# Weight blocks stored two by two, column by column, and a pad tile of 64 instead of 128 bytes

## The chip, the cores and the metric

The kernel runs on one core of one Trainium2 chip. The metric is the device time of one execution in microseconds (us). The profile names five engines: PE (TensorE, the matrix unit, whose weight loads have a row PEld of their own), DVE (VectorE), ACT (ScalarE), POOL (GpSimd) and SP (SyncE, which here only issues DMAs).

## The reference, cut to what matters

Two transformer-like blocks of two layers each, on 256 tokens of width 1024, all in float32. What matters for this change is that nearly all the work is the product of activations with large weight matrices:

```python
for l in range(2):                                   # first block
    proj = rmsnorm(x, ...) @ w_in[l]                 # 1024 -> 6656: q k v g, conv inputs, gates
    y_ret, y_sc, y_cf = retention(...) @ w_ret_out[l], conv3(...) @ w_sc_out[l], conv31(...) @ w_cf_out[l]
    x = x + rmsnorm((g0*y_ret + g1*y_sc + g2*y_cf) @ w_o[l], ...)
    gate, val = split(conv3(rmsnorm(x, ...) @ w_up[l]))       # 1024 -> 2 * 2816
    x = x + rmsnorm((silu(gate) * val) @ w_down[l], ...)      # 2816 -> 1024
for l in range(2):                                   # second block
    z = rms(x, ...) @ w_in_2[l]                      # mLSTM, sparse attention, differential attention, gates
    x = x + merged(...) @ w_out_2[l]
    x = x + (silu(g) * u) @ w_down_2[l]              # g, u = split(rms(x, ...) @ w_gate_up_2[l])
```

## The kernel before, in words

Activations lie transposed: 128 partitions hold 128 features, and the 256 tokens run along the free dimension. All weights are cut on the host into blocks of 128 by 128, in the very order in which the kernel uses them (`plan`, `pack_weights`), and packed into one array `stream` of chunks of eight blocks (128 x 1024 float32, 512 KB). `Weights` loads a chunk into `wraw` by one DMA on SP's queue (line 307). ACT rounds it into `whi` (float32r, line 326), and DVE forms the rest `wlo = wraw - whi` (line 328, recorded at line 417). Four buffers each of `wraw`, `whi` and `wlo`.

`job` walks over the plan. For a job of kind "B" each weight block is the stationary operand and the 256 tokens of one slice of the activations move past it: three matmuls of 128x256 a block (whi with the high part of the activations, whi with the low part, wlo with the high part: `hh`/`hl`, `yh`/`yl`, `fh`/`fl` in the profile), each with its own weight load, summed in PSUM. Four chunks (`WHOLE`) are used as plain float32, with one matmul a block that shows as two instructions. For a job of kind "A" (the values v, mv, dv and the up-projected values of the sparse attention) the roles are turned round: the activations are loaded and four weight blocks move past, 512 columns at once; it takes four blocks together (`take(4)`), kind "B" takes them singly:

```python
    def take(self, n=1):
        c, b = divmod(self.cur, CB)
        assert b + n <= CB
        self.cur += n
        s = slice(b * P, (b + n) * P)
        return [y[:, s] for y in self.parts[c]]
```

So before, block b of a chunk is the contiguous 128 columns b*128 to b*128+127 (512 bytes in each partition), and consecutive columns of the block are 4 bytes apart.

The order of the instructions on each engine comes from a scheduler that sees the jobs and, between them, side tasks (convolutions, attention, norms) which `side` hands out by estimated PE and DVE time. Tiles are given addresses in the order in which the pools are made: weights, constants, then the pool "state" (`xpool`), whose first tile `xpad` (line 365) is never used; its 128 bytes only move what is allocated after it: `x`, `hh`, `hl`, `yh`, `yl` and all pools behind. As the built program has them, every weight block of `whi`, `wlo` and `wraw` begins 128 bytes after a multiple of 256, and every slice of `hh`, `hl`, `yh`, `yl`, `fh`, `fl` begins 64 bytes after one.

Of the kernel before, what the change touches and what calls it, by code (L numbers as in the profile page):

```python
# [11 lines left out]
F32 = mybir.dt.float32  # L12
# [5 lines left out]
P = 128  # L18
# [108 lines left out]
def pack_weights(inputs):  # L127
    blocks = []
    cache = {}
    for arr, idx, kind, nk, cols in plan():  # L130
        key = (arr, idx)
        if key not in cache:
            cache[key] = np.asarray(inputs[arr])[idx]
        w = cache[key]
        if kind == "B":
            c = np.concatenate(cols)
            t = w[:, np.maximum(c, 0)]
            if (c < 0).any():
                t = np.where(c[None, :] < 0, np.zeros_like(t), t)
            n = len(cols)  # L140
            blocks.append(t.reshape(nk, P, n, P).transpose(0, 2, 1, 3).reshape(nk * n, P, P))
        else:
            t = w[:, cols].reshape(nk, P, 4, P).transpose(0, 2, 1, 3).reshape(nk * 4, P, P)
            blocks.append(t)
    n = sum(b.shape[0] for b in blocks)
    tot = -(-n // CB) * CB
    out = np.zeros((tot // CB, P, CB, P), np.float32)
    i = 0
    for b in blocks:
        for j in range(b.shape[0]):  # L150
            out[(i + j) // CB, :, (i + j) % CB, :] = b[j]
        i += b.shape[0]
    return out.reshape(tot // CB, P, CW)
# [59 lines left out]
def make_consts():  # L213

    off, parts = {}, []
    pos = 0

    def add(name, a):
        nonlocal pos
        a = np.asarray(a, np.float32)  # L220
        if a.shape[0] < P:
            a = np.concatenate([a, np.zeros((P - a.shape[0],) + a.shape[1:], np.float32)])
        a = a.reshape(P, -1)
        off[name] = (pos, a.shape[1])
        pos += a.shape[1]
        parts.append(a)

    add("ident", np.eye(P))
    inv = (np.float32(1.0) / np.power(np.float32(10000.0), np.arange(0, 64, 2, dtype=np.float32) / np.float32(64))).astype(np.float32)
    ang = np.arange(T, dtype=np.float32)[None, :] * inv[:, None]  # L230
    cos = np.cos(ang.astype(np.float64)).astype(np.float32)
    sin = np.sin(ang.astype(np.float64)).astype(np.float32)
    add("cos", np.tile(cos, (4, 1)))
    add("sin", np.concatenate([-sin, sin, -sin, sin]))
    i = np.arange(P)
    add("causb", np.where(i[None, :] > i[:, None], NEG, 0.0))
    e4 = np.zeros((P, 4, 4))
    for h in range(4):
        e4[:, h, h] = 1.0 / P
    add("st4", e4)  # L240
    s8 = np.zeros((P, 4, 8))
    for t in range(4):
        s8[:64, t, 2 * t] = 1.0 / 64
        s8[64:, t, 2 * t + 1] = 1.0 / 64
    add("st8", s8)
    hm = np.zeros((P, 2))
    hm[:64, 0] = 1.0 / 64
    hm[64:, 1] = 1.0 / 64
    add("hm2", hm)
    sel = np.zeros((P, 3, 4))  # L250
    for h in range(4):
        sel[64 + h, 0, h] = 1.0
        sel[68 + h, 1, h] = 1.0
        sel[72 + h, 2, h] = 1.0 / 16
    add("sel", sel)
    return off, pos, np.concatenate(parts, axis=1)
# [26 lines left out]
class Weights:  # L283
# [5 lines left out]
    def __init__(self, g, stream):  # L289
        self.g, self.stream = g, stream  # L290
        self.n = stream.shape[0]
        self.raw, self.parts = {}, {}
        self.loaded = self.conv = 0
        self.cur = 0
        self.whole = whole_chunks()
        self.first = False
# [39 lines left out]
    def take(self, n=1):  # L336
        c, b = divmod(self.cur, CB)
        assert b + n <= CB
        self.cur += n
        s = slice(b * P, (b + n) * P)  # L340
        return [y[:, s] for y in self.parts[c]]


class Gen:
    SLACK = 4000

    def __init__(self, ctx, tc, aps):
        self.ctx, self.tc, self.nc = ctx, tc, tc.nc
        self.aps = aps
        nc = self.nc  # L350
        PS = bass.MemoryType.PSUM
        self.wpool = ctx.enter_context(tc.tile_pool(name="weights", bufs=1))
        self.cpool = ctx.enter_context(tc.tile_pool(name="consts", bufs=1))
        self.xpool = ctx.enter_context(tc.tile_pool(name="state", bufs=1))
        self.dram = ctx.enter_context(tc.tile_pool(name="dram", bufs=1, space=bass.MemoryType.DRAM))
        self.psum = ctx.enter_context(tc.tile_pool(name="psum", bufs=1, space=PS))
        self.jobs = iter(plan())
        self.norms = 0
        self.tasks, self.later = [], []
        self.pe = self.dve = 0  # L360
        self.t_x = [None]
        self.urgent = {}
        self.idle = None

        self.xpool.tile([P, 32], F32, name="xpad")
        self.x = self.xpool.tile([P, KD, T], F32, name="x")
        xin = aps["x"].rearrange("p (k t) -> p k t", k=KD)
        self.coff, nco, _ = make_consts()
        self.cst = self.cpool.tile([P, nco], F32, name="cst")
        self.poff, npr, _ = pack_params()  # L370
        self.prm = self.cpool.tile([P, npr], F32, name="prm")
        self.g0 = self.cpool.tile([P, KD], F32, name="g0")
        o = self.poff["norm_mix_pre", 0][0]
        nc.scalar.dma_start(self.g0, aps["params"][:, o:o + KD])
        self.ones = self.cpool.tile([P, T], F32, name="ones")
        nc.vector.memset(self.ones, 1.0)
        self.eps = self.cpool.tile([P, 1], F32, name="eps")
        nc.vector.memset(self.eps, EPS)
        self.warm = self.cpool.tile([P, 1], F32, name="warm")
        self.act(self.warm, self.eps, AF.Square)  # L380
        self.W = Weights(self, aps["stream"])
        for i in range(4):
            nc.sync.dma_start(self.x[:, 2 * i:2 * i + 2], xin[:, 2 * i:2 * i + 2])
            self.W.load_to(i + 1)
        nc.sync.dma_start(self.prm, aps["params"])
        nc.sync.dma_start(self.cst, aps["consts"])
# [1250 lines left out]
```

## Time and profile before

| | |
|---|---|
| time, median of 3 runs | 1784.51 us (1778.77 to 1785.51) |
| the profiled execution | 1783.79 us, of which span 1782.1 us |
| PE busy | 1770.8 us, 14462 matmul instructions |
| PEld busy | 1723.9 us, 14462 weight loads |
| DVE busy | 1360.8 us |
| ACT busy | 1110.6 us |
| POOL busy | 69.7 us |
[...]
| DMA | 322.52 MB, mean 181 GB/s |

A matmul's record runs from its start to a modelled end, and consecutive records overlap: one of 128x256 lasts about 0.28 us, yet they start some 0.115 us apart. What counts is therefore the distance from start to start, called the pace below, and not the duration or the busy share. A row of the chain of waits that merges many matmuls gives it: its time divided by its count.

### The profile page before, as it was taken

What the parts mean: (1) busy time and instruction counts of PE and PEld (TensorE: products, weight loads), DVE (VectorE), ACT (ScalarE), POOL (GpSimd) and SP (SyncE); (2) the same over time, 40 slices, a digit from 0 to 9 for tenths busy, and PEclk for the clock granted to TensorE, in tenths of its full rate; (3) what the DMA queues carried; (4) which work ended last, traced back from release to release, by engine and by line L of the source; (5) the groups of instructions that cost most, each with busy time, mean ns of one, the idle gap of its engine ahead of it and who ended that gap; (6) DMA issues with size and microseconds to landing.
All of it is one profiled execution on the core that took longest, in us unless ns stands there. A gap on an engine that the chain in (4) does not pass through costs nothing.

```text
span 1782.1 us, 35765 instructions
## 1 busy us (share of the span) xinstructions
PE 1770.8 (99%) x14462; PEld 1723.9 (97%) x14462; DVE 1360.8 (76%) x2082; ACT 1110.6 (62%) x1787; POOL 69.7 (4%) x144
## 2 busy tenths in 40 slices
PE   8999999999999999999999999999999999999999
PEld 8999999999999999999998999999999999999999
DVE  8998689866999779883988877855569887687553
ACT  7676568755666568764676666644457666655442
POOL 0000000000000000000022100000001210000000
PEclk9999999999999999999999999999999999999999
DMA  7655545555555545555555644555555664455553
GB/s 269 195 177 187 191 143 202 190 189 172 200 177 190 180 149 195 190 189 166 164 191 181 210 133 146 190 185 187 188 185 172 202 196 137 144 188 189 188 189 121
DMA packets 94648, 322.52 MB, mean 181 GB/s; under 512 B 12257, under 2 KB 16913, under 8 KB 94482
## 3 DMA queue, kind: packets, MB, share of 16 engines
q1 hardware_dynamic: 91010, 314.15, 53.1%
q0 software_dynamic: 3328, 6.09, 1.2%
q8 instruction: 113, 1.85, 0.4%
q14 instruction: 53, 0.43, 0.1%
q10 hardware_dynamic: 144, 0.00, 0.0%
HBM read 312.80 MB, written 1.10 MB: 176 GB/s over the span
## 4 chain that ended last, share of the span: by engine, by line
PE 97%; DVE 1%; DMA 1%; issue 1%; ACT 0%; POOL 0%; SPq 0%; DVEq 0%; ACTq 0%; POOLq 0%
PE acc L405 90%; PE sp L405 6%; PE sp L410 1%; DMA Wm<-rows 0%; DMA tmp<-dq 0%; DMA x<-x 0%; DVE sc L1169 0%; DVE x L417 0%; DVE m L1168 0%; DVE yw L422 0%; DVE wlo L417 0%; ACT sd L447 0%; DVE dq L417 0%; ACT whi L326 0%; DVE Wm L428 0%
## 5 line engine op out<-in xcount | busy, mean ns | idle before, releaser
L326 ACT ACTIVATE whi<-wraw 128x1024 fp32r<-128x1024 f32 (+1 forms) x575 | 606.5, 1057 | 529.6 <-PE acc L405 359.6
L417 DVE TENSOR_TENSOR wlo<-wraw,whi 128x1024 fp32r<-128x1024 f32 (+1 forms) x575 | 697.0, 1218 | 285.9 <-ACT whi L326 284.8
L405 PE MATMUL acc<-hh,whi 128*128 128x256 f32 x2832 | 791.4, 280 | 0.0
L405 PE MATMUL acc<-hl,whi 128*128 128x256 f32 x2832 | 791.0, 280 | 0.0
L405 PE MATMUL acc<-hh,wlo 128*128 128x256 f32 x2832 | 789.8, 280 | 0.0
L405 PEld LDWEIGHTS acc<-hh,whi 128*128 128x128 f32 x2832 | 534.0, 189 | 5.5 <-issue 3.7
L405 PEld LDWEIGHTS acc<-hh,wlo 128*128 128x128 f32 x2832 | 534.4, 189 | 1.1 <-issue 0.8
L405 PEld LDWEIGHTS acc<-hl,whi 128*128 128x128 f32 x2832 | 532.0, 188 | 1.9 <-issue 1.2
L405 PE MATMUL acc<-yh,whi 128*128 128x256 f32 x1280 | 268.5, 283 | 6.1 <-ACT whi L326 6.1
L405 PE MATMUL acc<-yh,wlo 128*128 128x256 f32 x832 | 230.8, 282 | 0.0
L405 PEld LDWEIGHTS acc<-yh,whi 128*128 128x128 f32 x1280 | 210.4, 190 | 6.9 <-ACT whi L326 6.1
L405 PE MATMUL acc<-fh,wlo 128*128 128x256 f32 x704 | 197.9, 281 | 0.0
L405 PE MATMUL acc<-fl,whi 128*128 128x256 f32 x704 | 197.7, 281 | 0.0
L405 PE MATMUL acc<-fh,whi 128*128 128x256 f32 x704 | 197.5, 281 | 0.0
L405 PEld LDWEIGHTS acc<-yh,wlo 128*128 128x128 f32 x832 | 156.7, 190 | 0.4
L405 PEld LDWEIGHTS acc<-fh,wlo 128*128 128x128 f32 x704 | 133.6, 190 | 0.0
L405 PEld LDWEIGHTS acc<-fh,whi 128*128 128x128 f32 x704 | 133.5, 190 | 0.0
L405 PEld LDWEIGHTS acc<-fl,whi 128*128 128x128 f32 x704 | 132.2, 188 | 0.0
L405 PE MATMUL acc<-yl,whi 128*128 128x256 f32 x384 | 107.5, 281 | 0.0
L405 PEld LDWEIGHTS acc<-yl,whi 128*128 128x128 f32 x384 | 72.2, 188 | 0.2
L447 ACT ACT_TABLE_LOAD x50 | 64.2, 1283 | 5.3 <-DVE Wm L428 2.8
L422 DVE SCALAR_TENSOR_TENSOR up<-z,prm,up 128x254 f32<-128x254 f32 (+1 forms) x128 | 55.1, 476 | 0.0
(282 smaller groups left out, 1812.1 us busy)
## 6 DMA issues: line engine op xcount, KB each, us to landing
wraw<-stream SPq DMA_DIRECT2D x581, 512.0 KB, 3.4
kr<-rows SPq DMA_DIRECT2D x32, 64.0 KB, 3.1
dec<-decay SPq DMA_DIRECT2D x2, 768.0 KB, 4.2
x<-x SPq DMA_DIRECT2D x4, 256.0 KB, 6.2
rf<-rows SPq DMA_DIRECT2D x8, 128.0 KB, 3.6
tmp<-dq POOLq DMA_DIRECT2D x16, 64.0 KB, 2.9
Wm<-rows SPq DMA_DIRECT2D x8, 128.0 KB, 3.2
tmp<-dk POOLq DMA_DIRECT2D x16, 64.0 KB, 4.0
```

The lines of the kernel that those rows point to most:

```text
L326: nc.scalar.activation(h[:, s], r[:, s], AF.Copy)
L405: return self.nc.tensor.matmul(out, lhsT, rhs, start=start, stop=stop, **kw)
L410: return self.nc.tensor.transpose(out, in_, self.c("ident")[:k, :k])
L417: self.recent = self.nc.vector.tensor_tensor(out=out, in0=a, in1=b, op=op)
L422: return self.nc.vector.scalar_tensor_tensor(out, a, s, b, op0=op0, op1=op1)
L447: return self.nc.scalar.activation(out, in_, f, **kw)
```

## The change

Three edits.

1. `pack_weights` lays the blocks of kind "B" out in pairs: in the 256 columns that two consecutive blocks take up, column 0 of the first block is followed by column 0 of the second, then column 1 of each, and so on. Blocks of kind "A" stay as they were. The bytes, chunks and DMAs are the same.
2. `take`, when it hands out a single block, gives every second column of the pair: 128 columns that are 8 bytes apart, spread over 1024 bytes instead of 512. The second block of a pair begins 4 bytes after the first.
3. The unused tile `xpad` has 64 bytes instead of 128, so that everything behind it moves down by 64 bytes. The slices of `hh`, `hl`, `yh`, `yl`, `fh`, `fl` now begin at a multiple of 256; the weight buffers stay where they were. From the start of the weights to the start of the activations it was 192 bytes modulo 256; it is 128 for the first block of a pair and 124 for the second.

In the compiled program a weight load's pattern starts at the last column of the block and steps down: by one element before, by two now. The moving operand steps up by one element in both.

No engine's instructions change their order, their number or their waits: on PE, DVE, ACT, POOL and SP the lists of both programs agree row by row, up to line numbers.

```diff
@@ pack_weights @@
             n = len(cols)
-            blocks.append(t.reshape(nk, P, n, P).transpose(0, 2, 1, 3).reshape(nk * n, P, P))
+
+            t = t.reshape(nk, P, n, P).transpose(0, 2, 1, 3).reshape(nk * n // 2, 2, P, P)
+            blocks.append(t.transpose(0, 2, 3, 1).reshape(-1, P, 2, P).transpose(0, 2, 1, 3).reshape(-1, P, P))
@@ Weights.take @@
         self.cur += n
+        if n == 1:
+
+            s = slice((b & ~1) * P, (b | 1) * P + P)
+            return [y[:, s].rearrange("p (c h) -> p h c", h=2)[:, b & 1] for y in self.parts[c]]
         s = slice(b * P, (b + n) * P)
         return [y[:, s] for y in self.parts[c]]
@@ Gen.__init__ @@
-        self.xpool.tile([P, 32], F32, name="xpad")
+        self.xpool.tile([P, 16], F32, name="xpad")
```

## Rows read from the trace of the kernel before

**Rows 1.** The page: busy time of the engines, and the chain's shares
```profile
PE 1770.8 (99%) x14462; PEld 1723.9 (97%) x14462; DVE 1360.8 (76%) x2082; ACT 1110.6 (62%) x1787; POOL 69.7 (4%) x144
PE 97%; DVE 1%; DMA 1%; issue 1%; ACT 0%; POOL 0%; SPq 0%; DVEq 0%; ACTq 0%; POOLq 0%
```

**Rows 2.** The chain of waits, merged pieces: start us, us, what, count
```profile
113.00 43.18 PE acc L405 x379
...
165.13 66.31 PE acc L405 x563
...
246.80 177.61 PE acc L405 x1508
...
533.46 50.66 PE acc L405 x445
...
593.51 58.06 PE acc L405 x493
...
667.05 177.61 PE acc L405 x1508
...
1135.80 173.37 PE acc L405 x1472
...
1545.23 51.59 PE acc L405 x455
...
1599.29 179.15 PE acc L405 x1521
```

**Rows 3.** The page's costliest groups: matmuls of kind "B", count, busy us, mean ns
```profile
L405 PE MATMUL acc<-hh,whi 128*128 128x256 f32 x2832 | 791.4, 280 | 0.0
L405 PE MATMUL acc<-yh,whi 128*128 128x256 f32 x1280 | 268.5, 283 | 6.1 <-ACT whi L326 6.1
L405 PE MATMUL acc<-yh,wlo 128*128 128x256 f32 x832 | 230.8, 282 | 0.0
L405 PE MATMUL acc<-fh,wlo 128*128 128x256 f32 x704 | 197.9, 281 | 0.0
L405 PE MATMUL acc<-yl,whi 128*128 128x256 f32 x384 | 107.5, 281 | 0.0
```

**Rows 4.** Groups of PE from 560 to 580 us
```profile
L405 PE MATMUL acc<-hh,whi 128*128 128x256 f32 x59 | 16.1, 276 | 0.0
```

**Rows 5.** Groups of PE from 700 to 720 us
```profile
L405 PE MATMUL acc<-hh,whi 128*128 128x256 f32 x57 | 16.0, 281 | 0.0
```

**Rows 6.** Timeline from 1007.5 us: sixteen weight loads, each with a matmul of 2 columns
```profile
1007.42 1.87 PEld L405 LDWEIGHTS sp<-cst,sqt 128*128 128x128 f32 x16
1007.53 1.84 PE L405 MATMUL sp<-cst,sqt 128*128 128x2 f32 x16
```

**Rows 7.** Timeline of PE from 425 us: plain float32 matmuls (start us, us)
```profile
425.54 1.46 PE L405 MATMUL acc<-ones 128*128 128x256 f32 x6
```

**Rows 8.** Timeline of PE from 44 us: kind "A", 512 columns (start us, us)
```profile
44.04 0.39 PE L405 MATMUL acc<-whi,hh 128*128 128x512 f32 x1
...
46.33 0.39 PE L405 MATMUL acc<-wlo,hh 128*128 128x512 f32 x1
```

**Rows 9.** Windows: us, busy us of PE, PEld, DVE, ACT, POOL, clock, DMA share, GB/s
```profile
260.00:440.00 180.00, 179.75 (x1481) 178.00 (x1481) 136.90 (x217) 121.93 (x206) 0.20 (x1) 1.00 0.54 183
440.00:480.00 40.00, 40.00 (x296) 37.89 (x296) 38.79 (x56) 26.84 (x40) 3.93 (x8) 1.00 0.63 209
480.00:600.00 120.00, 120.00 (x1026) 117.75 (x1025) 113.97 (x160) 76.84 (x112) 0.51 (x1) 1.00 0.56 182
860.00:900.00 40.00, 39.99 (x294) 37.35 (x292) 38.22 (x59) 25.05 (x36) 4.02 (x8) 1.00 0.62 203
1320.00:1360.00 40.00, 40.00 (x315) 38.46 (x314) 37.54 (x58) 25.76 (x35) 3.99 (x8) 1.00 0.59 197
```

**Rows 10.** The page's costliest groups: forming `whi` and `wlo`
```profile
L326 ACT ACTIVATE whi<-wraw 128x1024 fp32r<-128x1024 f32 (+1 forms) x575 | 606.5, 1057 | 529.6 <-PE acc L405 359.6
L417 DVE TENSOR_TENSOR wlo<-wraw,whi 128x1024 fp32r<-128x1024 f32 (+1 forms) x575 | 697.0, 1218 | 285.9 <-ACT whi L326 284.8
```

## The prediction, written before the changed kernel ran

> **What bounds the kernel now.** I read the page's busy shares and the chain's shares first. PE holds 97% of the chain and is busy for 99% of the span [rows 1], so only what changes PE's pace or gives it a wait can change the time. The page's busy time cannot say how much, since records of matmuls overlap. So I read the merged pieces of the chain next [rows 2], and then the starts of the matmuls one after the other.
>
> There are 13152 matmuls of kind "B" in float32r: the groups of 2832 (three of them), 1280, 832, 704 (three) and 384 [rows 3], and 48 on the compressed key-value slice. Six long pieces of the chain, 563 + 1508 + 493 + 1508 + 1472 + 1521 = 7065 matmuls, take 832.1 us, which is a pace of 117.8 ns; three others, 1279 matmuls, take 145.4 us, at most 113.7 ns each with the end of the last record still in it [rows 2]. Start by start the picture is sharper: of the 13028 distances between neighbours of this kind, 4445 lie at 112 to 114 ns (mean 113.33), 8403 at 116 to 120 ns (mean 117.78), and only 180 elsewhere. Two paces, nothing between, and a stretch keeps its pace for up to 1508 matmuls while DVE, ACT and the DMAs come and go. So the pace is not set by those engines' traffic but by something PE does with itself, and it is restarted when another kind of matmul interrupts the stream. A record lasts 276 ns in a fast stretch [rows 4] and 281 ns in a slow one [rows 5]: the lost time lies within the matmul.
>
> How fast could it be? Two rows give floors. Weight loads with nearly nothing moving (2 columns) follow each other every (1.87 - 0.19) / 15 = 112.0 ns [rows 6]. Plain float32 matmuls of 256 columns, in two instructions each, come every (1.46 - 0.38) / 5 = 216 ns [rows 7]; there the columns move at half the rate, and if 256 columns of float32r need half of it, they need 108 ns. So the stream could run at the loads' 112 ns; it loses 1.3 ns in the fast stretches and 5.8 in the slow ones. Kind "A" shows a loss as well: (46.33 - 44.04) / 10 = 229 ns for 512 columns [rows 8], against 216 by the same reckoning.
>
> What fits all this, and what I assume: the stream loses time when a load and the moving operand want the same part of the memory at once. The load walks 512 bytes down while the activations walk 1024 bytes up, so that they meet at changing places, and how a stretch begins decides how often. Plain float32, with its slower columns, has the time to give way and loses nothing. [...]
>
> **The change part by part.** *Order, counts, DMAs.* Nothing moves on any engine, so no wait is added and none taken away. Cost 0, and no cover is needed.
>
> *The spread load.* Each of the 13152 loads now walks 1024 bytes in the time in which the activations walk 1024. No row shows a load with a step other than one. From below: a load cannot make the pair faster than 108 ns, which would be 8403 x 9.8 + 4445 x 5.3 = 106 us less. From above: if a load's time goes with the bytes that it spans, 112 becomes 224 ns, and 13152 x (224 - 116.2) = 1418 us more (116.2 is the mean over both paces). The row that it is nearest to is [rows 6]: the same 128 columns, contiguous. I take 112 ns, the load's time unchanged.
>
> [...]
>
> *The distance.* With both walks at the same rate and in opposite directions, load and activations either meet in every second turn or never, by where they begin. [...] I take the loss to be gone: the pace falls to the load's 112.0 ns in all stretches, 8403 x 5.78 + 4445 x 1.33 = 48.6 + 5.9 = 54.5 us.
>
> *Kind "A".* 288 matmuls, whose loads stay contiguous; their distance moves from 64 to 128. At most 288 x 13 = 3.7 us either way; I take 0.
>
> *What is late next.* A chunk feeds 24 matmuls, 2.69 us at 112 ns; forming it takes ACT 1.06 and DVE 1.22 us [rows 10], and its 512 KB need 195 GB/s, where windows of 203 and 209 are in the trace [rows 9]. In the long stretch 260 to 440 us DVE is busy for 136.9 of 180 us, so 80% of the shortened one. But DVE has 38.8 of 40 us around 440, 38.2 of 40 around 860, 37.5 of 40 around 1320 and 114.0 of 120 from 480 to 600 [rows 9]: there PE can gain 3 to 5%, which is about what it is to gain, and now and then it will wait. I take 2 us off.
>
> *Sum.* 54.5 - 2 = 52.5 us; 1783.8 (the profiled execution) - 52.5 = 1731.3. The median of the runs lies 0.7 us above that execution: 1732.
>
> **Rivals.**
> 1. *A meeting is left at the start of each load.* Load and activations need not begin at the same instant, so the walks may not be quite in step; one short stall each time brings them in step, and everything runs at the fast pace known from before, 113.3. For it: the fast pace is so stable. Against: the stall might hide in the 4 ns by which the load (112) is slower than the columns (108). 8403 x 4.44 = 37.3 us less: 1747.
> 2. *Nothing happens.* The two paces come from something other than the load's address, for instance PSUM, which isn't touched. For it: the trace shows no address. Against: the durations differ within the matmul while its output is the same kind in both. 1784.5. [...]
> 3. *Slower: the spread load collides more.* It fetches from twice as many places. If each fetch can hold up the activations, and the walks are out of step by enough that they meet after all, the loss over 108 ns doubles: 5.3 becomes 10.6 and 9.8 becomes 19.6, 8403 x 9.8 + 4445 x 5.3 = 106 us more, 1890. Mildest, the stream keeps to the slow pace everywhere: 4445 x 4.44 = 19.7 us more, 1804. It decides from a mean pace of 116.2 ns upwards. For it: no row has a strided load. Against: a load by itself has 112 ns in [rows 6] and would have to slow down or push.
>
> [...]
>
> **How the numbers follow.** Forecast 0.46, rival 1 0.21, rival 2 0.11, rival 3 0.22, of which a quarter near its mild end. The forecast's own range is 1715 to 1742: below, kind "A" gains its 3.7 us and the load proves 1 ns faster than the rounded row; above, DVE's tight windows cost 10 us. The range that should hold 8 in 10 takes in rivals 1 and 2 and the mild end of 3: 1713 to 1804. What a measurement of this kernel can tell from no change is 0.5%, 9 us. Faster by more: forecast and rival 1, 0.67; within: 0.11; slower by more: 0.22.
>
> **What would show it.** In the profile after, the long pieces of the chain (1508, 1508, 1472, 1521) should take 169 us instead of 177.6 at the first and show one pace in all stretches, with records of kind "B" at 276 ns or less. Weight loads should keep their 0.19 us. If pieces still show 113.3 and 117.8 ns in turns, the assumption on the meeting is wrong (rival 2); if the pace is one and above 118, rival 3 holds, and if loads last longer as well, it's the load's own time. If PE's pace falls but its busy share too, DVE's tight windows have taken the gain.

## The result, and the profile after

The change made the kernel slower: 1838.59 us (median of 4 runs, 1838.40 to 1839.87) against 1782.06 us before (4 runs, two of them near 1779 and two near 1785 us); the ratio is 1.0319, with a 95% interval of 1.0294 to 1.0343. The forecast was 1732, and its range ended at 1804.

The page of the changed kernel, busy time and the chain's shares by engine and by line (lines of the program have moved by six: L411 is L405 of before):

```profile
PE 1826.5 (99%) x14462; PEld 1780.2 (97%) x14462; DVE 1365.0 (74%) x2082; ACT 1111.5 (60%) x1787; POOL 69.7 (4%) x144
PE 98%; DMA 0%; DVE 0%; ACT 0%; issue 0%; SPq 0%; DVEq 0%
```

Against [rows 1], DVE, ACT and POOL have the same work, and PE has 56 us more. It is still the chain. So the time went into PE, and the chain shows no new wait. The chain's merged pieces, start us, us, what, count:

```profile
117.90 46.10 PE acc L411 x379
173.20 67.56 PE acc L411 x563
256.29 180.96 PE acc L411 x1508
...
1171.86 176.63 PE acc L411 x1472
1592.70 55.11 PE acc L411 x455
1650.31 184.22 PE acc L411 x1521
```

These are the pieces of [rows 2], matmul for matmul. The piece of 1508 ran at 177.61 / 1508 = 117.8 ns and now runs at 180.96 / 1508 = 120.0; the piece of 379, which was a fast one, went from 43.18 to 46.10 us, which is from 113.3 to 121.1 ns with the first start and the last record taken off. The fast pace of before is gone, and the slow one is slower: the stretches now run at 120.0 or at 121.1 ns. Start by start: the 13028 times from one start to the next, between neighbours of kind "B", add up to 1584.7 us, where before they added up to 1529.8. These 54.8 us are all but 1.2 us of the 56.0 us by which the span grew (1782.1 to 1838.1).

The page's groups, matmuls of kind "B" and their weight loads (the number behind the comma is the mean ns of one), and below them the loads of the kernel before:

```profile
L411 PE MATMUL acc<-hh,whi 128*128 128x256 f32 x2832 | 803.3, 284 | 0.0
L411 PEld LDWEIGHTS acc<-hh,whi 128*128 128x128 f32 x2832 | 550.4, 195 | 5.5 <-issue 3.7
L411 PEld LDWEIGHTS acc<-yh,whi 128*128 128x128 f32 x1280 | 216.7, 196 | 7.0 <-ACT whi L328 6.3
```
```profile
L405 PEld LDWEIGHTS acc<-hh,whi 128*128 128x128 f32 x2832 | 534.0, 189 | 5.5 <-issue 3.7 <-DVE sc L1169 0.4 <-ACT mv L447 0.4
```

A matmul takes 284 ns where it took 280 [rows 3], and, more telling, a weight load takes 195, where it took 189 and the forecast wanted it to keep its 0.19 us. That is the sign which the prediction had named for "the load's own time".

### The profile page after: what moved, and what is told of

It is laid out like the page before. It is cut to its first block, busy times and chain, and to the rows that moved or that the text cites. A ratio compares the mean times of both kernels' runs of the same rounds, so it can differ in the third digit from the quotient of the medians.

```text
span 1838.1 us, 35765 instructions
## 1 busy us (share of the span) xinstructions
PE 1826.5 (99%) x14462; PEld 1780.2 (97%) x14462; DVE 1365.0 (74%) x2082; ACT 1111.5 (60%) x1787; POOL 69.7 (4%) x144
## 4 chain that ended last, share of the span: by engine, by line
PE 98%; DMA 0%; DVE 0%; ACT 0%; issue 0%; SPq 0%; DVEq 0%
PE acc L411 92%; PE sp L411 6%; PE sp L416 1%; DMA Wm<-rows 0%; DMA x<-x 0%; DVE x L423 0%; DVE yw L428 0%; ACT sd L453 0%; DVE Wm L434 0%; SPq L566 0%; DVE wlo L423 0%; ACT yh L453 0%; ACT sqt L453 0%; DVE Wm L428 0%; ACT Wm L453 0%
## 5 line engine op out<-in xcount | busy, mean ns | idle before, releaser
L411 PE MATMUL acc<-hh,whi 128*128 128x256 f32 x2832 | 803.3, 284 | 0.0
L411 PE MATMUL acc<-hh,wlo 128*128 128x256 f32 x2832 | 802.5, 284 | 0.0
L411 PE MATMUL acc<-hl,whi 128*128 128x256 f32 x2832 | 802.1, 284 | 0.0
L411 PEld LDWEIGHTS acc<-hh,whi 128*128 128x128 f32 x2832 | 550.4, 195 | 5.5 <-issue 3.7
L411 PEld LDWEIGHTS acc<-hl,whi 128*128 128x128 f32 x2832 | 550.4, 194 | 1.9 <-issue 1.2
L411 PEld LDWEIGHTS acc<-hh,wlo 128*128 128x128 f32 x2832 | 549.2, 194 | 1.1 <-issue 0.8
L411 PE MATMUL acc<-yh,whi 128*128 128x256 f32 x1280 | 275.7, 287 | 6.3 <-ACT whi L328 6.3
L411 PE MATMUL acc<-yh,wlo 128*128 128x256 f32 x832 | 234.2, 286 | 0.0
L411 PEld LDWEIGHTS acc<-yh,whi 128*128 128x128 f32 x1280 | 216.7, 196 | 7.0 <-ACT whi L328 6.3
L411 PE MATMUL acc<-fh,wlo 128*128 128x256 f32 x704 | 199.6, 284 | 0.0
L411 PE MATMUL acc<-fl,whi 128*128 128x256 f32 x704 | 198.6, 282 | 0.0
L411 PE MATMUL acc<-fh,whi 128*128 128x256 f32 x704 | 198.3, 282 | 0.0
L411 PEld LDWEIGHTS acc<-yh,wlo 128*128 128x128 f32 x832 | 160.6, 195 | 0.3
L411 PEld LDWEIGHTS acc<-fh,whi 128*128 128x128 f32 x704 | 136.7, 194 | 0.0
L411 PEld LDWEIGHTS acc<-fl,whi 128*128 128x128 f32 x704 | 136.2, 193 | 0.0
L411 PEld LDWEIGHTS acc<-fh,wlo 128*128 128x128 f32 x704 | 136.0, 193 | 0.0
L411 PE MATMUL acc<-yl,whi 128*128 128x256 f32 x384 | 109.3, 285 | 0.0
L411 PEld LDWEIGHTS acc<-yl,whi 128*128 128x128 f32 x384 | 75.0, 195 | 0.1
```

The costliest lines, as they stand in the source:

```text
L411: return self.nc.tensor.matmul(out, lhsT, rhs, start=start, stop=stop, **kw)
```

## The experiments

Each expectation defines the theories that it names. All ratios compare with the kernel before on the same chip. "Distance" stands below for bytes alone: from the start of the weights to the start of the activations, modulo 256.

**1 to 3: the edits apart.** Edits 1 and 2 alone (pairs, with `xpad` as before, so that the distance from the weights to the activations is 192 or 188 bytes modulo 256); edit 3 alone; and the pairs at a third distance, 0 or 252.

```diff
 e_pairs_pad128: edits 1 and 2 as in the change, and
         self.xpool.tile([P, 32], F32, name="xpad")
 e_plain_pad64: pack_weights and take as before, and
-        self.xpool.tile([P, 32], F32, name="xpad")
+        self.xpool.tile([P, 16], F32, name="xpad")
 e_pairs_pad192: edits 1 and 2 as in the change, and
-        self.xpool.tile([P, 32], F32, name="xpad")
+        self.xpool.tile([P, 48], F32, name="xpad")
```

Expected of the pairs with the old pad:

> The paired layout alone, with the pad of before (distance 192 and 188 instead of 128 and 124). Theory A (the load with a step of two columns costs more wherever the activations begin): slower than before, 1825 to 1850 us, paces of 119 to 122 ns, loads of 194 to 196 ns. Theory B (the pairs are harmless, the new distance is what costs): 1775 to 1790 us with the paces 113 and 118. Theory C (pairs with the right distance help, with the wrong one hurt; 128 was the wrong one): clearly faster than before, 1720 to 1760.

Expected of the small pad alone:

> The pad of 64 bytes alone, blocks contiguous as before (distance 128). Theory A: near the kernel before, 1765 to 1800 us, since the load is the old one. Theory B: near the changed kernel, 1830 to 1845 us.

Expected of the pairs with the large pad:

> The paired layout with a pad of 192 bytes: the activations begin at the same place modulo 256 as the weights (distance 0 and 252). Theory A: 1825 to 1850 us again. [...]

| | load's step | distance | us (median) | ratio, 95% interval | neighbours of kind "B", start to start, sum |
|---|---|---|---|---|---|
| before (beside runs 1 to 3) | 4 bytes | 192 | 1784.8 | | 1529.8 us |
| after | 8 | 128, 124 | 1838.6 | 1.0319 (1.0294 to 1.0343) | 1584.7 |
| pairs, old pad | 8 | 192, 188 | 1833.4 | 1.0271 (1.0256 to 1.0286) | 1578.2 |
| pairs, large pad | 8 | 0, 252 | 1831.8 (2 runs) | 1.0263 (1.0242 to 1.0283) | 1578.6 |
| small pad alone | 4 | 128 | 1822.8 | 1.0213 (1.0196 to 1.0230) | 1567.3 |

One piece of the chain, the same 1508 matmuls in each, first of the pairs with the old pad, then of the pairs with the large one, then of the small pad alone:

```profile
254.93 180.96 PE acc L411 x1508
```
```profile
255.84 180.96 PE acc L411 x1508
```
```profile
254.05 178.95 PE acc L405 x1508
```

The pairs run at 120.0 ns at both of these distances; only at 128, in the changed kernel, some stretches ran at 121.1. The old layout at the new distance has two paces again, 118.7 in this piece and 120.0 in others, and its loads keep 189 ns. Both runs of pairs came out as theory A says, and the large pad, 1831.8 us, came out beside the old one (1833.4) and not at the 1838.6 us of the distance 128. The small pad alone missed both theories: 1822.8 us lies between them. So either half of the change is a loss by itself: the spread load costs 49 us, and the new distance, under contiguous loads, 38 us. They don't add up, because a stream that has the spread load no longer depends much on the distance: three distances lie within 7 us.

**4: the pace by itself.** A kernel, executed once, that holds nothing but stretches of 48 matmuls in an otherwise idle core, each with its own layout of the load, its own number of moving columns and its own distance, with six plain float32 instructions between them.

```diff
+                    s = w[:, b * step * P:(b + 1) * step * P]
+                    if step > 1:
+                        s = s.rearrange("p (c h) -> p h c", h=step)[:, half]
+                    o = dist // 4 + i // 6 % 3 * 512
+                    last = nc.tensor.matmul(ps[:, :cols], s, m[:, o:o + cols], start=i == 0, stop=i == N - 1)
```

> Nothing of the reference but its input x is kept: stretches of 48 matmuls, each with its own load, for loads with a step of one, two and four columns, moving operands of 2, 256 and 512 columns, and distances from 0 to 224 in steps of 32; each stretch twice, after plain float32 matmuls of 256 and of 50 columns. Theory A, in its form that the load itself is slower: loads of step two with 2 moving columns follow each other every 118 to 121 ns against 112 for step one, and with 256 columns all distances lie at 118 to 122. Theory A, in its form that only the meeting is dearer: 112 for both alone, and with 256 columns a pace that depends on the distance. A step of four (one column in 16 bytes): 112 if a load's time goes by columns, 125 to 230 if by places touched. Plain float32r with step one: 113 to 118 at a distance of 192, as in the kernel.

Its chain: "plain" is a step of one and "pair" a step of two; the letters a, c, e, g are distances of 0, 64, 128 and 192. Start us, us, what, count:

```profile
67.92 5.76 PE plain_e_x L64 x48
...
94.64 5.46 PE plain_g_x L64 x48
...
120.84 5.76 PE pair_a_x L64 x48
...
174.82 5.81 PE pair_e_x L64 x48
...
201.93 5.76 PE pair_g_x L64 x48
```

The mean of the last 24 start-to-start times of each stretch, in ns (two stretches each; two numbers where they differ):

| distance (bytes) | 0 | 32 | 64 | 96 | 128 | 160 | 192 | 224 |
|---|---|---|---|---|---|---|---|---|
| step one | 120.0 | 116.7 | 117.8 | 120.0 | 120.0, 118.8 | 117.4, 118.7 | 113.3 | 118.3 |
| step two | 120.0 | 120.8, 120.0 | 120.0 | 120.2, 120.1 | 121.1 | 120.0, 120.8 | 120.0 | 120.0 |

The core does nothing else here, and the paces of the two full kernels come out: 113.3 at 192 for the old layout, 121.1 at 128 for the new one. No other engine and no DMA is needed for them. The kernel before stood at the one distance of these eight where contiguous loads do best, and there is none at which pairs come below 120.0. A step of four gave 233.3 ns. Loads with 2 moving columns were in the same kernel, but the granted clock fell behind them (0.53 on average from 580 to 600 us, 0.50 from 606 us to the end), and a step of one and of two took 213.3 ns alike; hence the next run. A step of four took 233.3 ns at a granted clock of 0.50 too, so its time did not go with TensorE's clock.

One thing these runs leave out: in the programs as built, the weights begin 128 bytes after a multiple of 256 here as in the full kernels, and only the activations move. So whether it is the distance that counts, or where the activations lie by themselves, was not separated; "distance" names what was changed. Nor do the two places keep their order for every shape: with 512 moving columns and contiguous loads it turns round, 226.7 ns at 0 and 233.3 at 192.

**5: the load alone at full clock, the distance in steps of 8 bytes, and what interrupts a stretch.** This kernel, too, was executed once. 90 matmuls go ahead of each group of loads, and the granted clock in the windows of the four groups shown was 1.00, 1.00, 1.00 and 0.99; for steps of three and four the blocks of weights are taken further apart. The other stretches start at distance 192, and after 24 matmuls one matmul of another shape interrupts them.

```diff
+        stream("warm", 0, 90, 192, 90)
+        stream("alone_" + name, 0, 18, 0, 18, cols=2, step=step)
```

> Nothing of the reference but its input x is kept: (1) stretches of 48 matmuls with contiguous loads at distances from 0 to 248 in steps of 8; (2) at the distance 192 of the kernel before, streams of 66 matmuls into which after 24 one odd matmul is put (2 to 224 moving columns, or a load of only 4 or 64 columns); (3) loads of step one, two, three and four columns with 2 moving columns, each after a warm stream. [...] For (1): the pace is a multiple of a few ns that depends on the distance, 113.3 at 192 and 116 to 120 elsewhere; a distance below 113.3 would be news. For (2): if the slow pace of the kernel before (117.8 at the distance 192) is only how a stretch starts, some odd matmuls bring 113.3 and some 117.8 behind them, always the same for one kind; if it needs the kernel's other engines, all are at 113.3.

The chain of this kernel: eighteen loads with 2 moving columns each, at steps of one to four:

```profile
384.52 1.90 PE alone_one L67 x18
...
398.00 2.01 PE alone_two L67 x18
...
412.84 3.01 PE alone_three L67 x18
...
427.04 4.09 PE alone_four L67 x18
```

From start to start they take 111.67, 117.78, about 174 and 233.3 ns; a second group of steps one to three gave 111.67, 117.8 and 175. That settles the load: a step of two isn't free, it costs 6.1 ns on top of 112, and at steps of two to four the time went with the bytes spanned (117.78 / 2, 174 / 3 and 233.3 / 4 are 58 to 59 ns per 512 bytes). In steps of 8 bytes no distance gave contiguous loads less than 113.3 ns. One besides 192 reached it, 112; the one stretch at 192 in that row of 32 stood at 117.8.

So at distance 192 a stretch starts at 113.3 or at 117.8 ns, also in an idle core. Behind the same two plain float32 matmuls of 256 columns, 17 stretches of this kernel at 192 started at 113.3 and 8 at 117.8, so that the kind of what goes ahead does not decide alone. What interrupts a stretch can change 113.3 into 117.8; the other way round did not happen in this kernel (first 24 and then 42 matmuls of a stretch; the interruption is a float32r matmul of 96 columns, then of 192 columns, then a plain float32 matmul with a load of 4 columns):

```profile
261.37 2.73 PE kick_e L67 x24
264.15 5.01 PE kick_e L67 x42
...
287.36 2.75 PE kick_h L67 x24
290.19 4.79 PE kick_h L67 x42
...
304.31 2.74 PE kick_few_a L67 x24
...
307.17 4.97 PE kick_few_a L67 x42
```

All three stood at 113.3 ahead of the interruption; the steady paces behind it are 117.8, 113.3 and 113.3 (the last piece is longer because its second start comes 222 ns after the first). All five stretches behind a plain matmul with a small load stood at 113.3, as they had ahead of it.

**6 and 7: choose the pace in the kernel before.** If such a matmul also brings a stretch from 117.8 to 113.3, the slow stretches of before can be switched. One plain float32 matmul with a load of 4 columns was put at 16 places (the first gate job of each branch, one job in each feed-forward stage); it writes to an accumulator that the next matmul starts afresh. As a control, a short float32r matmul of the stream's own kind at the same places.

```diff
 e_kicks
+            if kick:
+                with self.tc.issue_after(self.last_mm.ins):
+                    self.mm(accs[0][:4, :2], self.ones[:, :4], self.ones[:, :2])
 e_same_kind
+                    if kick and k == 0 and t == 0:
+                        self.mm(accs[0][:, :2], ws[0], xs[0][:, :2])
```

> The kernel before (contiguous loads, distance 192), with one plain float32 matmul of a 4-column load and 2 moving columns put in at 16 places: at the first gate job of each of the 12 branches and at one job inside each of the 4 feed-forward stages. Theory B (at distance 192 the stream has two steady paces, and the kind of matmul that interrupts it chooses): behind such a matmul every stretch known so far runs at 113.33 ns, so the long pieces of the chain that ran at 117.78 fall to 113.33 from that place on; some 5600 to 6100 matmuls x 4.44 ns = 25 to 27 us less, against 16 x 0.33 = 5 us for the added matmuls: 1758 to 1768 us. Rival (the pace is set by the stage, by its operands' addresses or by what the other engines do in it): the pieces stay at 117.78 and the added matmuls cost 5 us: 1786 to 1792 us.

> The control: at the same 16 places the added matmul is of the stream's own kind, float32r with the full load of 128 contiguous columns and 2 moving columns. Theory B, with what the measurement of single stretches showed (a stretch at 117.78 keeps its pace behind such a matmul): the pieces stay at 117.78, 16 x 0.17 = 3 us are added, 1784 to 1791 us. Rival (any short matmul restarts the stream at its fast pace): as with the plain one, 1756 to 1768 us.

The control gave 1791.5 us, ratio 1.0046 (1.0031 to 1.0060): as expected and a little more. All nine pieces of over 100 matmuls behind an added one ran at 117.8 ns: those that had this pace before kept it, and those at 113.3 lost it. The piece of 445, in which the added matmul stands, took 50.66 us [rows 2] and now takes this:

```profile
534.38 51.64 PE acc L405 x445
```


The plain matmuls gave 1811.5 us, ratio 1.0156 (1.0139 to 1.0173), and so missed both theories. The pieces did what theory B says, in part: of the ten pieces of over 100 matmuls behind an added one, eight ran at 113.3 ns (at six of these places the pace had been 117.8, and four of them switched), and two of the four in the feed-forward stages landed in 117.8 again. The neighbours of kind "B" add up to 1515.8 us, 14.0 less than before. What was won there was lost elsewhere. PE's waits (what it waited for: us in total, times, longest), and two windows of 60 us (busy of PE, PEld, DVE, ACT, POOL, clock, DMA share, GB/s):

```profile
PE sp L411 <- DVE prob L423: 21.3, 2, 11.0
...
PE sp L405 <- DVE dk L418: 3.6, 1, 3.6
```
```profile
940.00:1000.00 60.00, 43.46 (x281) 37.76 (x282) 43.74 (x82) 33.05 (x82) 14.51 (x32) 0.77 0.41 132
1420.00:1480.00 60.00, 49.10 (x306) 42.57 (x307) 43.27 (x78) 35.45 (x84) 13.06 (x28) 0.83 0.48 150
```

In the attention stages of the second block the added matmuls had moved side work on PE, which now waits twice for DVE's `prob`, 21.3 us in all; and around each wait the granted clock is at 0.50 for a while, 27.3 us the first time and 20.5 the second (0.77 and 0.83 on average in these windows; it was 1.00 in both windows of the kernel before), with matmuls 213 ns apart.

**8 to 10: the same without moved work.** First all 16 again, but left out of the program's own count of PE time; then only the four in the feed-forward stages, where no attention work runs beside; then these four with two matmuls of 256 columns each.

```diff
-                    self.mm(accs[0][:4, :2], self.ones[:, :4], self.ones[:, :2])
+                    for _ in range(1):
+                        self.nc.tensor.matmul(accs[0][:4, :2], self.ones[:, :4], self.ones[:, :2], start=True, stop=True)
 e_ffn_short: besides, no kick in the gate jobs
 e_ffn_long: as e_ffn_short, with range(2) and 256 columns
```

> The same 16 plain float32 matmuls (4-column load, 2 moving columns), but left out of the program's own count of PE time, so that all other PE instructions keep the order of the kernel before. In the run with counted ones the long pieces fell to 113.33 ns where the kick took, but two of the four long feed-forward pieces landed in 117.78 again, and a changed order of the attention work made PE wait (11 us at one place, with the granted clock at half speed around it). Theory B: without the changed order the gain of the faster pieces shows: 14 to 25 us less at the pieces, 5 us for the added matmuls, and at most 5 us for attention work that is now late: 1763 to 1780 us. Rival (the faster PE itself runs ahead of DVE and ACT in the attention stage, so that what is gained is waited for there): the pieces fall, but PE waits as much: 1784 us or more.

> Four of them alone, one inside each feed-forward stage, uncounted. Theory B: the 1390 matmuls behind each run at 113.33 instead of 117.78, 6.2 us each, in two stages (as with the counted ones) to four: 12 to 25 us less, 1.3 us for the added ones: 1761 to 1774 us. Rival (what is gained is waited for elsewhere, or the pace does not follow the kind): 1784 to 1786 us.

> The same four places with two plain float32 matmuls of a 4-column load and 256 moving columns each, the kind behind which every stretch of the kernel before stood at 113.33 ns. Theory B, if the kind of the interrupting matmul decides whatever the stretch before it did: all four long pieces fall to 113.33, 25 us less, 4 x 0.8 = 3 us for the added ones: 1762 us. Rival (the phase in which the stretch before it stood decides as well): one or two pieces stay at 117.78, 1768 to 1775 us.

The 16 uncounted ones gave 1811.4 us, as slow as the counted ones. The expectation's premise was wrong: the count was not what moved the work. PE's order is the same as with the counted matmuls, row by row of the trace, and 411 of its 14462 rows stand elsewhere than before; the same wait for `prob` is there, 21.3 us. What moved them stays open.

With the four alone PE's order in the trace is that of before, row by row. The single ones gave 1773.7 us, ratio 0.9937 (0.9921 to 0.9954), the pairs 1766.4, ratio 0.9910 (0.9886 to 0.9934). The pieces behind them, of the single ones:

```profile
261.17 157.98 PE acc L405 x1392
...
675.57 157.98 PE acc L405 x1392
...
1141.50 158.38 PE acc L405 x1343
...
1604.94 164.17 PE acc L405 x1392
```

157.98 / 1392 is 113.5 ns, the first starts included; 164.17 / 1392 and 158.38 / 1343 are 117.9. Two of four switched, worth 2 x 6.2 us; less 1.3 for the added matmuls that makes 11.1, and the medians differ by 10.8. With the pairs the fourth switched as well (157.99 us for its 1392) and the third did not. That is the traced execution, which with 1774.7 us was the slowest of the four of this version: against the single ones it lost again what the fourth stage had won, with 3.4 us at a granted clock of 0.50 around 948 us (0.96 on average from 940 to 980 us) and a stretch of 337 matmuls before the third stage that ran at 117.8 instead of 113.3. What the faster ones did (1764.3 to 1767.1 us) was not traced.

**11: a second try four jobs later.** The pair as in e_ffn_long, and 192 matmuls behind it one with 2 columns.

```diff
-                    self.job(evac, mov, kick=i == 4)
+                    self.job(evac, mov, kick={4: 256, 8: 2}.get(i))
```

> The pair of 256-column plain float32 matmuls at the four feed-forward places, and at each four jobs later (192 matmuls) one plain matmul of a 4-column load and 2 moving columns as a second try. With the pair alone three of four long pieces fell to 113.33 and the one of the third stage kept 117.78. Theory B with the phase (whether a stretch at 117.78 is switched depends on where it stands when it is interrupted; one at 113.33 stays there behind such a matmul): a second try switches the third stage for its last 1150 to 1200 matmuls in about half of the cases, 5.2 us, and costs 4 x 0.33 us: 1762 to 1769 us. Rival (the third stage is slow for a reason of its own, its operands' addresses or what the other engines do in it): it keeps 117.78, and the time is 1767 to 1769 us.

1768.0 us, ratio 0.9921 (0.9902 to 0.9939). The third stage switched at the second try; its two pieces on the chain:

```profile
1145.01 22.82 PE acc L405 x192
...
1167.95 130.67 PE acc L405 x1151
```

22.82 / 192 is 118.9 ns with the first starts in it, 130.67 / 1151 is 113.5. In the other three stages the second matmul left the pace at 113.3. So the third stage is not slow for a reason of its own; why one plain matmul switches a slow stretch and another doesn't stays open. By time, the three versions with four places can hardly be told apart (their ranges overlap), and 1768.0 us fits theory and rival alike, so that the trace alone decides here; all three beat both kernels. The best median is that of the pairs of 256 columns, 0.9% below the kernel before and 4% below the changed one.

## Why the prediction was wrong, point by point

- *What bounds the kernel.* Right. PE's pace alone set the time: 54.8 of 56.0 us lie between the starts of neighbours of kind "B", and the chain shows no added wait.
- *The spread load*, "I take 112 ns, the load's time unchanged". This is the step that failed. By itself such a load takes 117.78 ns. With that the fast pace can't exist any more, which alone is 4445 x (117.78 - 113.33) = 19.8 us. The other 35 us come from the stream's running at 120.0 to 121.1 and not at its load's 117.78; that these go with the spread load is shown (runs 1, 3 and 4), how they arise is not. In the same way the contiguous load, 111.67 alone, gives 113.33 at best. The bounds of the term, 108 and 224 ns, held the true value; the choice within them fell on the nearest row, which had a load of another step. The lower bound, 108, was an estimate, half of the 216 ns of [rows 7]; the least that a steady stretch of 256 float32r columns took in any run is 113.3. The measurement decides: a step of two loses 6.1 ns, and a step of four takes about twice the time of a step of one, 233.3.
- *The distance*, "I take the loss to be gone". Wrong as well. No run shows the 54.5 us of this term, and that load and activations hinder each other where they meet was the author's assumption, which no run tested. What the runs showed in its place: with the spread load the pace hardly asks for the distance (120.0 ns at 192 and 0, 120.0 and 121.1 at 128), so there was nothing to win; and with contiguous loads the old distance of 192 is the best of the eight, and 128 costs 38 us. That the pace depends on where the activations lie, under the same load, was right (113.3 at 192, 118.8 and 120.0 at 128); that their place relative to the load is what counts was not tested, nor whether places 256 bytes apart are alike. Which distance is good was not to be had from the trace.
- *Kind "A"*, 0 (±3.7 us). Within its bounds: the 295 start-to-start times between neighbours of this kind add up to 69.1 us in the changed kernel and to 68.6 before. There are 312 such matmuls, not 288; the sum had left out the 24 on the compressed key-value slice.
- *What is late next.* Not tested by this change, since PE got no faster. Where PE did get faster in the feed-forward stages (runs 9 to 11), hardly anything new waited (1.1 us at the most at one place). The windows quoted for it leave PE up to 6% (37.5 of 40 us), not 5. DVE became the bound only where work had been moved (runs 6 and 8).
- *The rivals.* Rival 3 came true, in the form that the signs at the end named, "the load's own time" (with two paces, 120.0 and 121.1, both above 118). Its price of 1804 to 1890 us holds the result; its mild end, everything at 117.8, was too mild, and the range was cut there. Rival 1, everything at 113.3, is what runs 9 to 11 reach in the feed-forward stages, by another way. Rival 2 did not come: edits 1 and 2 alone, which change where the loads read and nothing else, took the fast and the slow pace to 120.0 ns and cost 49 us (run 1). The runs also show that place counts under the same loads: with the same 256 columns the pace is 113.3 or 120.0 ns by where the activations lie, and with 512 columns the same two places come in the other order (233.3 and 226.7). No run has these matmuls without their loads.

What stays open: why a stream with spread loads needs 2 to 3 ns more than its loads alone, why, with contiguous loads and 256 columns, a distance of 192 is good and 0 bad (113.3 and 120.0 ns), and what decides whether a slow stretch is switched. The runs show all three as facts and none of them as a mechanism.

## What to carry to other kernels

Here the weight loads follow each other closely (PEld is busy for 97% of the span [rows 1]), and their layout was part of the pace (111.67 ns alone at a step of one, 117.78 at a step of two, and 49 us of the kernel): measure the load by itself, with few moving columns and the clock up, before its stride is traded for anything else. Two sharp paces in one trace (113.3 and 117.8 ns), kept over hundreds of matmuls, meant here that a stretch keeps the pace it has until an interruption changes it; it can then be cheaper to restart it than to rearrange the data. Such an insertion paid here only where the order of everything else stayed: matmuls of this kind won 0.6 to 0.9% in the feed-forward stages and lost 1.6% when the attention work had moved as well.

## What the runs showed of the hardware that was not expected

- The time of a load of 128 float32r columns by its step, at a granted clock of 1.00 (0.99 for the last): 111.67, 117.78, 174 to 175 and 233.3 ns for steps of 4, 8, 12 and 16 bytes; at a granted clock of 0.50 the last is 233.3 ns as well, while the first two are both 213.3.
- With the weights at one place modulo 256 bytes, the pace of float32r matmuls of 256 columns with contiguous loads goes by where the activations lie: of 32 distances in steps of 8 bytes, about half gave 120 ns, 112 gave 113.3 and three gave about 121; 192 gives 113.3 or 117.8. The paces of the idle core are those of the full kernels: 113.3 and 117.8 at 192 with contiguous loads, 121.1 at 128 with the spread ones.
- At a distance of 192 there are two steady paces, 113.33 and 117.78, and a stretch of up to 1508 matmuls keeps the one it started in. A float32r matmul of 96 to 160 columns moved a stretch from 113.33 to 117.78, one of 192 or 224 columns left it at 113.33 (in the full kernel one of 2 columns, too, moved it to 117.78); a plain float32 matmul with a load of 4 columns left every stretch at 113.33 there and, in the full kernel with 16 of them, moved four of six stretches at 117.78 to 113.33.
- A wait of 11 us in a PE-bound kernel cost more than itself: the granted clock stood at 0.77 and 0.83 on average over the 60 us around two such waits. That run is 26.9 us slower although its pace won 14.0; the waits (36.2 us in PE's list of waits against 7.7 before, so 28.5 more) and the added matmuls (16 x 0.33 = 5) leave some 7 us. PE worked for 27.3 us in the two stretches at a clock of 0.50, where matmuls start 213 ns apart, so up to half of that, about 14 us, is an estimate of the most that the clock can have cost.
